# One hybrid decoder layer on one core: the values step of two head pairs is put one tick later

## The chip, the cores and the metric

The kernel runs on one core of a Trainium2 chip. The metric is the device time of one execution in microseconds (us). Five engines matter here: PE (TensorE, the matrix engine), ACT (ScalarE), DVE (VectorE), POOL (GpSimd) and SP (SyncE, which does nothing here but issue transfers). Transfers go through two queues that the profile counts: q1 holds what SP issues, q0 what POOL issues.

## What is computed

One decoder layer on 256 positions of width 2048, in float32. Two kinds of attention with 16 heads each read slices of one projection, and each head has 64 columns:

```python
q_a, k_a, v_a, q_b, k_b, v_b, f_b = jnp.split(rmsnorm(x, pre_mix_g) @ w_in, cuts, axis=-1)
# group A: causal window of 128, 2 key heads for 16 query heads, ALiBi, a learned sink per head
p = jnp.exp(s - m); p = p / (jnp.sum(p, -1) + jnp.exp(sink - m)); o_a = p @ v_a
# group B ("fox"): causal, with per-head forget gates
c = lax.cumsum(log_sigmoid(f_b + b_forget), axis=1)
s = q_b @ k_b.T * scale + c[t] - c[s];  o_b = softmax(s) @ v_b
mix = concatenate([rmsnorm(o_a, grp_swa_g), rmsnorm(o_b, grp_fox_g)]) @ w_out
x = x + rmsnorm(mix, post_mix_g)
# then a feed-forward block of width 5632 with a short causal convolution:
x = x + rmsnorm((gelu(gate) * val) @ w_down, post_ffn_g)
```

## The kernel before

**Numbers.** Each float32 operand of a product is split into a high part and the rest (`hi`, `lo`, names that end in `h`, `l` or `hi`, `lo`), and a product is three matmul passes: high by high, high by low, low by high. ACT makes the high part with a copy, DVE the rest with a subtraction. A 512 KB weight tile is loaded by SP (`raw`, five buffers), cast by ACT (`whi`, L168) and completed by DVE (`wlo`, L171). A `raw` buffer is free for the next load when its `wlo` has been made, so SP's queue of loads follows DVE.

**Order of the work.** PE's order is written out by hand: it is the order in which the program calls. The other engines' instructions are placed by the scheduler of the tile framework. Attention is interleaved with the projections: `proj_T` (matmuls at L309 and L314) calls `tick()` four times in each half of a projection (after the third and the sixth high step, in the pass of the low parts, and at the end), and `later(n, f)` puts a step off by n ticks. What falls on one tick is called in the order in which it was registered.

**A head pair.** `attend` makes four steps for two heads at a time: `tables` (POOL writes the additive mask into `p`; in the fox group this needs a load `cb` of the summed gates), `scores` (PE, L531, three passes with the split keys in `keys`; then DVE maxima, ACT exponentials, DVE normalisation into `p`), `transposes` (PE turns `p` round, L566, three 128x128 blocks for each of the two heads; ACT then casts `ph` and DVE subtracts `pl`, L368 and L369), and `pv`, the values step (PE multiplies by the values, L578 and L580 in the first group, L590 and L592 in the fox group; ACT and DVE bring the result to `oT`, and its squares in `sqo` are added up by POOL, L607 or L609). `ph` and `pl` have one buffer each: the next pair's may be written once this pair's values step has read them. The four steps take their PSUM banks with the tag `att` from four buffers in turn.

**The stages.** Pairs are taken two at a time, m = 0 and 1. `stages(n, m)` gives the ticks of scores, transposes and values: n, n+6+3m, n+9+4m. So the transposes of pair m = 1 and the values step of pair m = 0 fall on the same tick, n+9. The first group ("swa") has pairs 0 to 7 (g = 0 to 3), the fox group pairs 0 to 7 as well, which write `oT` 8 to 15.

**Between the groups.** The gates' running sum is made by PE (L721), copied by DVE (L724), written by SP to the tensor `c_dram` (L725) and read back by SP as `cb`, spread over the partitions (L634). POOL makes the fox tables from it (L639, L641, L645) and afterwards scales the first fox keys (L498); ACT and DVE split these (L368, L369, `keys`), and PE's first fox scores (L531) follow.

**Transfers on the side.** For the feed-forward block, the kernel builds sums of weight rows in DRAM during attention: SP copies rows to tensors `t` (L87, 1 MB each), and POOL adds other rows to them with accumulating transfers (L94, `accum_op`). POOL's instructions are taken in order, so an L94 that stands behind a waiting L609 is issued after it.

Of the kernel before, what the change touches and what calls it, by code (L numbers as in the profile page):

```python
# [34 lines left out]
def hybrid_layer(ctx: ExitStack, tc: tile.TileContext, x, pre_mix_g, w_in, b_forget, sinks,  # L35
# [16 lines left out]
    def bank(tag="acc"):  # L52
        return ps.tile([P, 512], F32, tag=tag, bufs=4, name="bank_" + tag)
# [245 lines left out]
    def proj_T(w, c0, banks):  # L299

        for v in (0, 2):
            parts = [w_split(w_load(w_rows(w, u * 4, 4, c0, 256), 4, 256), still=True)
                     for u in (v, v + 1)]
            steps = [(u, a) for u in range(2) for a in range(4)]

            def high(u, a):
                kt = (v + u) * 4 + a
                for m, b in enumerate(banks):
                    pe.matmul(b, parts[u][0][:, a, m * P:(m + 1) * P], hT[:, kt, :],  # L309
                              start=(kt == 0), stop=(kt == KT - 1))  # L310

            def low(u, a):
                for m, b in enumerate(banks):
                    pe.matmul(b[:, 256:512], parts[u][1][:, a, m * P:(m + 1) * P],  # L314
                              hT[:, (v + u) * 4 + a, 0:256], start=False, stop=False)

            for n, (u, a) in enumerate(steps[:-1]):
                high(u, a)
                if n in (2, 5):
                    tick()  # L320
            for n, (u, a) in enumerate(steps):
                low(u, a)
                if n == 4:
                    tick()
            high(*steps[-1])
            tick()
# [40 lines left out]
    def split(hi, lo, src):  # L367
        act.copy(hi, src)  # L368
        dve.tensor_tensor(lo, src, hi.bitcast(F32), op=ALU.subtract)  # L369

    with tc.tile_pool(name="mixp", bufs=1) as mp:
# [37 lines left out]
        def scratch():  # L409
            rot[0] += 1  # L410
            i = 6 + rot[0] % 10
            return scr[:, i * 256:(i + 1) * 256]
# [80 lines left out]
        def evac_sum(b, dst, row):  # L493

            c = scratch()
            act.copy(c, b[:, 256:512])
            dve.tensor_tensor(dst, b[:, 0:256], c, op=ALU.add)
            pool.tensor_tensor(dst, dst, row, op=ALU.mult)  # L498

        def q_pair(b):  # L500
            q = scratch()
            evac_sum(b, q, rowq)
            qh = ap.tile([P, 256], F32R, tag="qh", bufs=6, name="qh")
            ql = ap.tile([P, 256], F32R, tag="ql", bufs=6, name="ql")
            split(qh, ql, q)
            return qh, ql

        def k_pair(b, i):
            k = scratch()
            evac_sum(b, k, rowk)  # L510
            split(khi[i], klo[i], k)
# [106 lines left out]
        def swa_pair(p, q, at):  # L618
            def table(t):
                for e in range(2):  # L620
                    slope = 2.0 ** (-8.0 * (2 * p + e + 1) / H)
                    pool.tensor_scalar(t[:, e, 0:256], dist, -slope, None, op0=ALU.mult)
                    pool.tensor_scalar(t[:, e, 256:384], dist[:, P:256], -slope, None,
                                       op0=ALU.mult)

            attend(p, q, p // 4, lambda t: vpa[:, t, p // 4, :], table, 2 * p, True, at,
                   True)
# [3 lines left out]
        def fox_pair(p, q, ki, at):  # L631
            def table(t):
                cb = ap.tile([P, 2, 256], F32, tag="cb", bufs=2, name="cb")
                sp.dma_start(cb.rearrange("p e k -> p (e k)"),  # L634
                             c_dram[2 * p:2 * p + 2, :].rearrange("e k -> (e k)")
                             .partition_broadcast(P))
                for e in range(2):
                    h = 2 * p + e
                    pool.tensor_scalar(t[:, e, 0:256], cb[:, e, :], -1.0, cq[:, 1, h:h + 1],  # L639
                                       op0=ALU.mult, op1=ALU.add)  # L640
                    pool.tensor_scalar(t[:, e, 256:384], cb[:, e, 0:P], -1.0, cq[:, 0, h:h + 1],  # L641
                                       op0=ALU.mult, op1=ALU.add)

                v = t[:, :, P:384]
                pool.affine_select(out=v, in_=v, compare_op=ALU.is_ge, fill=NEG, base=0,  # L645
                                   pattern=[[0, 4], [-1, P]], channel_multiplier=1)

            attend(8 + p, q, ki, lambda hl, t: vpb[:, hl, t, p, :], table, 2 * p, False, at)

        def stages(n, m):  # L650
            return n, n + 6 + 3 * m, n + 9 + 4 * m


        def kv_a():
# [21 lines left out]
        for g in range(4):  # L676
            if g == 0:
                b2 = bq0
            else:
                b2 = [bank(), bank()]  # L680
                proj_T(w_in, g * 256, b2)
            for m in range(2):
                swa_pair(2 * g + m, q_pair(b2[m]), stages(7 + 8 * g, m))


        z = ap.tile([P, 2, H], F32, tag="z", name="z")
        for p0, npair, cols in ((0, 3, 384), (3, 3, 384), (6, 2, 272)):
            b2 = [bank(), bank()]
# [55 lines left out]
        for g in range(4):  # L744
            bq = [bank(), bank()]
            proj_T(w_in, 1280 + g * 256, bq)
            qs = [q_pair(b) for b in bq]
            bk = [bank(), bank()]
            proj_T(w_in, 2304 + g * 256, bk)
            for m in range(2):  # L750
                ki = (2 * g + m + 2) % NK
                k_pair(bk[m], ki)
                fox_pair(2 * g + m, qs[m], ki, stages(6, m))


        later(stages(6, 1)[2] + 4, lambda: group_rstd(1, rstd_b))
        mix_sb = main.tile([P, 2, D], F32, tag="y", name="mix_sb")
        mix = [[mix_sb[:, t, n * 512:(n + 1) * 512] for n in range(4)] for t in range(2)]
# [643 lines left out]
```

## Time and profile before

| what | value |
|---|---|
| median of 3 runs | 1056.29 us (1055.24 to 1056.49) |
| the profiled execution, its own time | 1056.47 us |
| its span in the trace | 1054.7 us, so 1.8 us lie around it |
| mean granted PE clock | 0.996 |
| PE busy | 1040.4 us, 99% of the span |
| DVE, ACT, POOL busy | 840.8, 660.5, 268.0 us |

The profiled execution stands 0.18 us above the median. Times inside the trace count from the start of the span. A row of the timeline gives the start, the length, the engine, the line, the operation, output and input, and how many instructions are taken together; in square brackets stands how long the engine was idle before it and what released it.

### The profile page before, as it was taken

To read this page: it belongs to the slowest core of one execution; us is meant where nothing else is said; L and a number is where in the kernel's file an instruction comes from. 1 tells how busy PE (TensorE), PEld (TensorE's weight loads), DVE (VectorE), ACT (ScalarE), POOL (GpSimd) and SP (SyncE) were. 2 spreads that over 40 slices of the span, in tenths; PEclk is the share of its full clock that TensorE was granted. 3 is DMA by queue.
4 is the path that set the end of the run, shared out by engine and by line. 5 is a ranking of instruction groups with operands and counts; after the bars stand their busy time and mean duration, and the time that the engine had idled before them with its cause. 6 is when DMAs were issued, how large, how long until landed. Compare 5 with 4: busy or idle time off the path is not lost.

```text
span 1054.7 us, 16573 instructions
## 1 busy us (share of the span) xinstructions
PE 1040.4 (99%) x5854; PEld 907.1 (86%) x5854; DVE 840.8 (80%) x1371; ACT 660.5 (63%) x1126; POOL 268.0 (25%) x312
## 2 busy tenths in 40 slices
PE   9999999999999999999999999999999999999996
PEld 7889988888889988888888888888888888888885
DVE  5988887787467888778877799867788788779996
ACT  6767666676655865566656675646555666567771
POOL 3254325442022224232232000013223223210004
PEclk9999999999999999999999999999999999999998
DMA  8978999988872899899999796899999999969893
GB/s 282 318 240 289 296 300 304 358 251 299 318 260 68 263 250 270 222 253 258 230 244 265 262 406 192 288 237 222 284 229 243 244 233 265 232 223 384 293 410 131
DMA packets 177470, 279.98 MB, mean 265 GB/s; under 512 B 9052, under 2 KB 133244, under 8 KB 176124
## 3 DMA queue, kind: packets, MB, share of 16 engines
q1 hardware_dynamic: 162432, 249.51, 69.3%
q0 software_dynamic: 13952, 26.74, 17.8%
q10 hardware_dynamic: 1004, 2.68, 0.6%
q8 instruction: 46, 0.75, 0.3%
q14 instruction: 36, 0.29, 0.1%
HBM read 274.55 MB, written 57.69 MB: 315 GB/s over the span
## 4 chain that ended last, share of the span: by engine, by line
PE 93%; DVE 2%; DMA 2%; POOL 1%; ACT 1%; issue 1%; SPq 0%; DVEq 0%; POOLq 0%; ACTq 0%
PE bank_acc L340 16%; PE bank_att L340 14%; PE bank_acc L365 12%; PE bank_att L1044 12%; PE bank_acc L346 8%; PE bank_acc L1044 7%; PE bank_att L346 7%; PE bank_acc L309 7%; PE bank_acc L314 4%; PE bank_att L531 1%; PE bank_att L566 1%; DMA gbc_ffn<-in_post_ffn_g_dram 1%; DVE wlo L171 1%; PE bank_acc L1002 1%; POOL y_sb L1307 1%
## 5 line engine op out<-in xcount | busy, mean ns | idle before, releaser
L171 DVE TENSOR_TENSOR wlo<-raw,whi 128x1024 fp32r<-128x1024 f32 (+3 forms) x271 | 334.2, 1245 | 94.6 <-ACT whi L168 86.9
L168 ACT CAST whi<-raw 128x1024 fp32r<-128x1024 f32 (+3 forms) x270 | 273.7, 1029 | 103.5 <-issue 45.0
L963 POOL TENSOR_TENSOR room<-room,rowf 128x256 f32<-128x256 f32 x88 | 95.8, 1109 | 331.6 <-DVE room L962 329.8
L340 PE MATMUL bank_acc<-hT,whi 128*128 128x512 f32 x736 | 173.3, 390 | 0.0
L340 PEld LDWEIGHTS bank_acc<-hT,whi 128*128 128x128 f32 x736 | 136.4, 188 | 27.4
L340 PE MATMUL bank_att<-hT,whi 128*128 128x512 f32 x640 | 150.6, 390 | 0.0
L340 PEld LDWEIGHTS bank_att<-hT,whi 128*128 128x128 f32 x640 | 118.7, 188 | 23.9
L967 ACT ACTIVATE room<-room,cw 128x256 f32<-128x256 f32 x88 | 52.5, 601 | 65.3 <-POOL room L963 65.0
L346 PEld LDWEIGHTS bank_acc<-hT,wlo 128*128 128x128 f32 x736 | 89.3, 188 | 2.0
L346 PE MATMUL bank_acc<-hT,wlo 128*128 128x256 f32 x736 | 89.8, 279 | 0.0
L309 PE MATMUL bank_acc<-hT,whi 128*128 128x512 f32 x352 | 88.0, 395 | 0.0
L1044 PE MATMUL bank_att<-whi,G 128*128 128x512 f32 x258 | 87.9, 389 | 0.0
L365 PE MATMUL bank_acc<-whi,oT 128*128 128x512 f32 (+1 forms) x272 | 81.8, 379 | 0.0
L369 DVE TENSOR_TENSOR wlo<-raw,whi 128x1024 fp32r<-128x1024 f32 (+1 forms) x66 | 71.4, 1102 | 10.3 <-ACT whi L368 9.6
L346 PEld LDWEIGHTS bank_att<-hT,wlo 128*128 128x128 f32 x640 | 77.6, 188 | 1.7
L346 PE MATMUL bank_att<-hT,wlo 128*128 128x256 f32 x640 | 77.9, 279 | 0.0
L973 DVE SCALAR_TENSOR_TENSOR room<-room,cw 128x256 f32<-128x256 f32 x88 | 59.2, 676 | 22.9 <-ACT room L967 22.9
L368 ACT CAST whi<-raw 128x1024 fp32r<-128x1024 f32 (+1 forms) x66 | 61.7, 953 | 23.2 <-issue 5.7
L309 PEld LDWEIGHTS bank_acc<-hT,whi 128*128 128x128 f32 x352 | 63.3, 188 | 11.6
L365 PEld LDWEIGHTS bank_acc<-whi,oT 128*128 128x128 f32 x272 | 50.2, 188 | 9.3
L1044 PEld LDWEIGHTS bank_att<-whi,G 128*128 128x128 f32 x258 | 48.4, 188 | 10.1
L365 PE MATMUL bank_acc<-wlo,oT 128*128 128x512 f32 (+1 forms) x136 | 51.2, 377 | 0.0
(269 smaller groups left out, 1757.3 us busy)
## 6 DMA issues: line engine op xcount, KB each, us to landing
raw<-in_w_up_dram SPq DMA_DIRECT2D x176, 512.0 KB, 5.6
raw<-in_w_in_dram SPq DMA_DIRECT2D x51, 512.0 KB, 6.4
raw<-in_w_down_dram SPq DMA_DIRECT2D x45, 512.0 KB, 6.9
raw<-in_w_out_dram SPq DMA_DIRECT2D x32, 512.0 KB, 7.0
t<-in_w_down_dram POOLq DMA_DIRECT2D x28, 512.0 KB, 9.2
raw<-t SPq DMA_DIRECT2D x26, 512.0 KB, 6.6
t<-t POOLq DMA_DIRECT2D x18, 512.0 KB, 8.6
extra<-t SPq DMA_DIRECT2D x14, 512.0 KB, 6.7
```

Of the source, the lines that this page charges most:

```text
L168: i1 = act.copy(hi[:, cs], raw[:, cs])
L171: i2 = dve.tensor_tensor(lo[:, cs], raw[:, cs], hi[:, cs].bitcast(F32), op=ALU.subtract)
L309: pe.matmul(b, parts[u][0][:, a, m * P:(m + 1) * P], hT[:, kt, :], start=(kt == 0), stop=(kt == KT - 1))
L340: pe.matmul(b, parts[u][0][:, a, m * P:(m + 1) * P], hT[:, kt, :], start=(kt == 0), stop=(kt == KT - 1))
L346: pe.matmul(b[:, 256:512], parts[u][1][:, a, m * P:(m + 1) * P], hT[:, kt, 0:256], start=False, stop=False)
L365: pe.matmul(b, a, r[:, cols], start=(first and i == 0), stop=(last and i == 2))
L368: act.copy(hi, src)
L369: dve.tensor_tensor(lo, src, hi.bitcast(F32), op=ALU.subtract)
L963: pool.tensor_tensor(u[:, 2:258], u[:, 2:258], rowf, op=ALU.mult)
L967: act.activation(y, u[:, 2:258], AF.Identity, bias=cw[:, 3, ch:ch + 1], scale=cw[:, 2, ch:ch + 1])
L973: dve.scalar_tensor_tensor(y, u[:, 1:257], cw[:, 1, ch:ch + 1], y, op0=ALU.mult, op1=ALU.add)
L1044: pe.matmul(b[:, to] if to else b, a, r[:, cols], start=(first and i == 0), stop=(last and i == 2))
```

## The change

`stages` takes one more argument, which puts the values step one tick later. It is set for pair m = 0 of the last swa group (g = 3, the seventh head pair) and for pair m = 0 of the first fox group (g = 0). One tick lies six or eight projection matmuls further on in PE's order.

```diff
-        def stages(n, m):
-            return n, n + 6 + 3 * m, n + 9 + 4 * m
+        def stages(n, m, more=False):
+            return n, n + 6 + 3 * m, n + 9 + 4 * m + more
...
             for m in range(2):
-                swa_pair(2 * g + m, q_pair(b2[m]), stages(7 + 8 * g, m))
+                swa_pair(2 * g + m, q_pair(b2[m]),
+                         stages(7 + 8 * g, m, g == 3 and m == 0))
...
-                fox_pair(2 * g + m, qs[m], ki, stages(6, m))
+                fox_pair(2 * g + m, qs[m], ki, stages(6, m, g == 0 and m == 0))
```

The changed file has one line more, so lines behind L683 carry a number one higher there.

PE, at the seventh swa pair. L309 and L314 are matmuls of the projection, L578 and L580 the values step of pair 6, L566 the transposes of pair 7:

```order
 L309 MATMUL bank_acc<-hT,whi 128x512 x2
+L566 MATMUL bank_att<-ident,p 128x128 x6
+L309 MATMUL bank_acc<-hT,whi 128x512 x6
 L578 MATMUL bank_att<-ph,vpa 128x512
 L578 MATMUL bank_att<-pl,vpa 128x512
 L580 MATMUL bank_att<-ph,vpa 128x2x128
 L580 MATMUL bank_att<-pl,vpa 128x2x128
-L566 MATMUL bank_att<-ident,p 128x128 x6
-L309 MATMUL bank_acc<-hT,whi 128x512 x14
+L309 MATMUL bank_acc<-hT,whi 128x512 x8
```

The transposes of pair 7 and six matmuls of the projection now stand ahead of the values step of pair 6.

PE, at the first fox pair. L590 and L592 are the values step of fox pair 0, L566 the transposes of fox pair 1:

```order
 L314 MATMUL bank_acc<-hT,wlo 128x256 x10
+L566 MATMUL bank_att<-ident,p 128x128 x6
+L314 MATMUL bank_acc<-hT,wlo 128x256 x6
+L309 MATMUL bank_acc<-hT,whi 128x512 x2
 L590 MATMUL bank_att<-ph,vpb 128x512 x2
 L590 MATMUL bank_att<-pl,vpb 128x512
 L592 MATMUL bank_att<-ph,vpb 128x2x128 x2
 L592 MATMUL bank_att<-pl,vpb 128x2x128
-L566 MATMUL bank_att<-ident,p 128x128 x6
-L314 MATMUL bank_acc<-hT,wlo 128x256 x6
-L309 MATMUL bank_acc<-hT,whi 128x512 x16
+L309 MATMUL bank_acc<-hT,whi 128x512 x14
```

The transposes of fox pair 1 and eight projection matmuls now stand ahead of the values step of fox pair 0.

The scheduler moves instructions of the other engines too. Two of these places are taken up below. First POOL, around the accumulating transfers into `t_74`:

```order
+L94 DMA t_74<-in_w_down_dram 256x512
 L609 TENSOR_TENSOR sqs<-sqs,sqo 128x256
 L94 DMA t_74<-in_w_down_dram 256x512
 L609 TENSOR_TENSOR sqs<-sqs,sqo 128x256 x2
-L94 DMA t_74<-in_w_down_dram 256x512
 L498 TENSOR_TENSOR scr<-scr 128x256 x2
```

There were three L609 around the first transfer, and the second transfer stood behind all of them; now both transfers stand ahead of the last two.

Second SP, around the write of the gates' sums (L725, which is L726 in the changed file) and the loads `cb`:

```order
 L113 DMA raw<-in_w_in_dram 128x4x256 x3
 L87 DMA t_89<-in_w_down_dram 16x16384
-L113 DMA raw<-in_w_in_dram 128x4x256
-L725 DMA c_dram<-scr 16x256
+L113 DMA raw<-in_w_in_dram 128x4x256 x2
+L726 DMA c_dram<-scr 16x256
 L113 DMA raw<-in_w_in_dram 128x4x256
 L634 DMA cb<-c_dram 128x512 x2
```

One weight load more now stands ahead of the write.

## The prediction

> **What bounds the kernel now.** I read the page first, then the list of what PE waited for, then the timeline of PE around the two values steps.
>
> ```profile
> PE 1040.4 (99%) x5854; PEld 907.1 (86%) x5854; DVE 840.8 (80%) x1371; ACT 660.5 (63%) x1126; POOL 268.0 (25%) x312
> PE bank_acc L390 <- DMA x_in<-in_x_dram: 1.3, 1, 1.3
> PE bank_acc L225 <- DVE junk L220: 1.3, 1, 1.3
> PE bank_att L590 <- DVE pl L369: 1.0, 1, 1.0
> PE bank_att L578 <- DVE pl L369: 0.5, 1, 0.5
> 240.00:860.00 620.00, 620.00 (x3417) 539.74 (x3416) 488.90 (x738) 378.55 (x596) 136.86 (x147) 1.00 0.88 253
> ```
>
> PE sets the time: it is busy 99% of the span, and the list names four waits in all. The first two are at the start. The other two are the values steps that the change moves: L590 (fox pair 0) and L578 (swa pair 6) wait for `pl`. The last row (a stretch of 620 us, PE busy in all 620) shows that PE has no gap for a long time behind them. So what PE gains before about 190 us is carried to the end, and so is what it loses.
>
> How large are the two stalls? The timeline of PE has each step disturbed, and some 9 us later the next pair's, which waits for nothing (start, length, what):
>
> ```profile
> 134.81 0.40 PE L578 MATMUL bank_att<-ph,vpa 128*128 128x512 f32 x1
> 135.75 0.50 PE L578 MATMUL bank_att<-pl,vpa 128*128 128x512 f32 x1 [0.54 <-DVE pl L369]
> 136.33 0.82 PE L566 MATMUL bank_att<-ident,p 128*128 128x128 f32 x6
> ...
> 144.38 0.40 PE L578 MATMUL bank_att<-ph,vpa 128*128 128x512 f32 x1
> 145.09 3.34 PE L309 MATMUL bank_acc<-hT,whi 128*128 128x512 f32 x14
> ...
> 179.90 0.63 PE L590 MATMUL bank_att<-ph,vpb 128*128 128x512 f32 x2
> 181.56 0.50 PE L590 MATMUL bank_att<-pl,vpb 128*128 128x512 f32 x1 [1.03 <-DVE pl L369]
> 182.26 0.82 PE L566 MATMUL bank_att<-ident,p 128*128 128x128 f32 x6
> ...
> 188.44 0.62 PE L590 MATMUL bank_att<-ph,vpb 128*128 128x512 f32 x2
> 189.49 0.87 PE L314 MATMUL bank_acc<-hT,wlo 128*128 128x256 f32 x6
> ```
>
> The swa step takes 136.33 - 134.81 = 1.52 us, undisturbed 145.09 - 144.38 = 0.71: it loses 0.81. The fox step takes 182.26 - 179.90 = 2.36, undisturbed 189.49 - 188.44 = 1.05: it loses 1.31. Together 2.12 us, 0.20% of the time. More cannot be gained, since the change removes no instruction.
>
> **Part 1: the swa step.** The transposes of pair 7 (0.57 us from start to start) and six matmuls of 0.235 us come first, so the values step starts about 2.0 us later, at 136.8. Its `pl` was there when PE went on at 135.75. The stall goes, and 0.81 us is gained. The transposes take the two banks behind those of pair 6, so they wait for nothing new. A few matmuls later PE needs the second weight tile of this half projection. It is sooner there by 0.81: transposes from 134.81, 0.57; six matmuls, 1.41; values, 0.71; two matmuls, 0.47; that is 137.97. ACT's cast of that tile:
>
> ```profile
> 136.75 1.03 ACT L168 CAST whi<-raw 128x1024 fp32r<-128x1024 f32 x1
> 124.12 0.37 SPq L113 DMA_DIRECT2D raw<-in_w_in_dram  x1
> raw<-in_w_in_dram SPq DMA_DIRECT2D x1, 512.0 KB, 9.3
> ```
>
> It ends at 137.78, 0.19 us ahead. The load behind this cast (five buffers back) is the one issued at 124.12; it landed 9.3 us later, at 133.4, so it has 3.3 us to spare.
>
> **Part 2: what happens to the 0.81 at the first fox scores.** These are the next place where PE comes close to an input. Rows of PE, ACT, DVE and POOL:
>
> ```profile
> 164.48 0.38 PE L531 MATMUL bank_att<-keys,qh 64*128 64x256 f32 x2
> 164.82 0.34 PE L531 MATMUL bank_att<-keys,qh 64*128 64x256 f32 x4
> 163.49 0.41 ACT L368 CAST keys<-scr 128x256 fp32r<-128x256 f32 x1 [5.80 <-POOL scr L498]
> 163.93 0.51 DVE L369 TENSOR_TENSOR keys<-scr,keys 128x256 fp32r<-128x256 f32 x1 [4.84 <-ACT keys L368]
> 162.72 1.44 POOL L498 TENSOR_TENSOR scr<-scr 128x256 f32<-128x256 f32 x2
> 157.17 0.48 POOL L639 TENSOR_SCALAR p<-cb,cq 128x256 f32<-128x256 f32 x1 [6.85 <-DMA cb<-c_dram]
> 151.81 0.82 SPq L634 DMA_DIRECT2D cb<-c_dram  x2
> 143.54 0.34 SPq L725 DMA_DIRECT2D c_dram<-scr  x1
> 164.50 2.94 ACT L168 CAST whi<-raw 128x1024 fp32r<-128x1024 f32 x3
> ```
>
> (The timeline prints the issues of SP with the queue's name; the others are engines.) The third pass of the scores, at 164.82, needs the low part of the keys, which DVE finishes at 163.93 + 0.51 = 164.44. That is 0.38 us to spare, some 0.33 with the 0.05 us by which PE started behind its release at 181.56. The keys wait for POOL, which works through the tables from 157.17 on, and these wait for `cb`, which waits for the write issued at 143.54. So PE can arrive only 0.33 us sooner, unless that chain is sooner too. Call D the shift of the chain (negative is sooner). After the scores PE is ahead by the lesser of 0.81 and 0.33 - D.
>
> **Part 3: the fox step.** Its own wait goes, but it is not lost from PE's path. The order puts the transposes of fox pair 1 at the place where the values step stood. Banks are taken in turn from four: pair 0's transposes take two, the group sum (L737) the third, so pair 1's first three blocks take the fourth and its second three the first again, which `pl` of pair 0 must have been read from. The row of DVE:
>
> ```profile
> 180.50 1.01 DVE L369 TENSOR_TENSOR pl<-bank_att,ph 128x384 fp32r<-128x384 f32 x2
> ```
>
> One of the two takes half, 0.5, so that bank is free at about 181.05, for PE at 181.10. PE would get there at 179.90 + 0.29 (three blocks of 0.095) = 180.19, less what it is ahead. Between POOL's L498 and this row ACT and DVE run in one chain of casts and exponentials (the last row above, from 164.50 on), so the row moves with D as well. With D = 0: PE is ahead by 0.33, arrives at 179.86 and waits 1.24 us. The values step itself comes eight matmuls later and waits no more. So of the 1.31 saved, 1.24 comes back at the transposes, and the total is 0.33 + 1.31 - 1.24 = 0.40. For other D the sum is 0.40 - D, up to the cap 2.12 (from D = -1.72 on).
>
> **Part 4: what the moved transfers do to D.** POOL's second accumulating transfer stood behind an L609 that waited 16 us for this very pair's squares:
>
> ```profile
> 141.03 0.73 POOL L609 TENSOR_TENSOR sqs<-sqs,sqo 128x256 f32<-128x256 f32 x1 [16.34 <-ACT sqo L602]
> 141.71 0.88 POOL L94 DMA_DIRECT2D t<-in_w_down_dram  x1
> ```
>
> It now goes out right behind the first, at about 119.7. What it did before is seen in the queues' rows for 146:150 (both queues), 137:141, 135:137 and 143:145 (packets, MB, share):
>
> ```profile
> q0 software_dynamic: 222, 0.45, 75.8%
> q1 hardware_dynamic: 230, 0.21, 21.7%
> ...
> q1 hardware_dynamic: 1190, 1.18, 96.1%
> ...
> q1 hardware_dynamic: 70, 0.12, 17.7%
> ...
> q1 hardware_dynamic: 173, 0.36, 45.9%
> c_dram<-scr SPq DMA_DIRECT2D x1, 16.0 KB, 8.3
> ```
>
> While q0 accumulates, SP's queue moves 0.21 MB in 4 us; alone it moves 1.18, 0.295 per us. The 0.21 would take 0.71 us, so the accumulation held SP's queue back by 3.29 us, and in this very time the 16 KB of `c_dram` took 8.3 us. This hold now falls into the time from 123 on, where it pushes weight loads back by as much; SP's queue was nearly idle at 135:137 (0.12 MB, that is 0.41 us of work in 2), which takes up 1.59, and again at 143:145 (0.36 MB, 1.22 us of work in 2), which takes up 0.78. There remain 0.92. And SP's order puts one load of 512 KB (0.524 MB, 1.78 us) ahead of the write. D = -3.29 + 0.92 + 1.78 = -0.59.
>
> What issues the write stays: DVE does the same work ahead of it in another order, and the row of that stretch shows it as good as full (17.57 of 18.5 us):
>
> ```profile
> 125.00:143.50 18.50, 17.96 (x115) 15.40 (x115) 17.57 (x50) 15.31 (x37) 1.56 (x2) 1.00 1.02 299
> ```
>
> The unknown is the transfers. From below, D is -3.29, if neither the load nor the early accumulation delays the chain. From above, it is -3.29 + 3.29 + 1.78 = 1.78, if the idle times of SP's queue take up nothing. I take -0.59, the sum of what the rows show, between the two.
>
> The Trainium skill, "DMA: Bandwidth & Descriptors", section "Latency and other measured facts", gives a transfer issued by SP about 0.6 us to its first byte and a trip to memory up to 2 us at high load; from that an estimate for a write of 16 KB that finds its rings empty is 2.6 us. By that page the write would be back 5.7 us sooner, D would pass its useful limit of -1.72 and the gain would be 2.12. The trace of before does not agree while loads and an accumulation stand in the queues (8.3 us), so I go by the rows; the page speaks for the rival of the full gain only.
>
> **Sum.** 0.40 + 0.59 = 0.99 us gained: 0.81 + 1.31 kept, less 1.13 (1.72 - 0.59) waited at the transposes, and nothing at the scores. 1056.47 - 0.99 = 1055.48 on the profiled execution's own time, which is 0.18 above the median: 1055.30. With the bounds of D the gain lies between 0.40 - 1.78 = -1.38 and 2.12, that is 1057.67 to 1054.17.
>
> **What else moves.** The values step of fox pair 0 is later, and with it everything that reuses `ph` and `pl`: pair 1's can be written only after it. PE would finish it at about 183.1 (181.10 - 0.59, three blocks, six L314 of 0.13, two L309, and 1.05). ACT and DVE then need two casts, two subtractions of 0.5 each and perhaps a `wlo` of 1.2 in between, some 3 us, so 186.1; pair 1's values step stands at 188.44 less the gain, at 187.45. It is hidden with 1.3 us to spare; without that cover PE would wait for `pl` again.
>
> **The rivals.** 0.2% is 2.1 us here: a measurement of this kernel cannot tell less from no change.
>
> *Full gain* (0.25): the chain is at least 1.72 us sooner. For it: the accumulation leaves the very stretch in which the write was slow. Against it: one load more ahead of the write, and loads that were pushed back before. 1056.29 - 2.12 = 1054.17, on the edge of what counts as faster.
>
> *Nothing* (0.15): D is about 0.2, so PE gains 0.2: the swa gain goes at the scores, the fox gain at the transposes. For it: both stalls have the same late `pl`, whatever PE does first. 1056.1.
>
> *Slower* (0.15): the transfers of the accumulation, issued while the weight load of 124.1 is in the queue, and the load ahead of the write delay the keys, and PE waits at the L531 scores, where it never waited. It decides from D = 0.40 on. With D = 1.78 the loss is 1.38: 1057.7. To be slower by 2.1 us, D would have to be 2.5. For it: 0.33 us to spare is little. Against it: the idle stretches of SP's queue.
>
> *The forecast* (0.45): gain 0.5 to 1.6, its own range 1054.7 to 1055.8, with 1055.3 as the middle.
>
> **How the numbers follow.** The range 1054.0 to 1057.5 holds the forecast, the full gain with the spread of the runs, no gain, and most of the slower case; about 0.07 lies below and 0.08 above. Faster by over 2.1 us: 0.11, a part of the full gain, which ends on this bound, and gains that I don't see. Slower by over 2.1 us: 0.07, the far half of the slower case. The rest, 0.82, is within.
>
> **What would show it.** Right: no wait of PE at L578; a wait at L566 for `pl` at about 179.4, of about 1.1 us; none at L590; POOL's second accumulation issued before 121 and q1 busier at 146:150; `cb` landing about 0.6 us sooner. Wrong: a wait of PE at L531 (chain later), a wait at L309 for `whi` near 138 (the pushed load), no wait at L566 at all (chain much sooner), or one of PE behind 190 us.

## The result

| kernel | median (lowest to highest), us | executions |
|---|---|---|
| before | 1056.29 (1055.24 to 1056.97) | 5 |
| changed | 1059.85 (1058.77 to 1061.16) | 5 |

The changed kernel is slower by 3.56 us: the ratio is 1.0037, with the interval 1.0026 to 1.0048. The forecast was 1055.3, with a range up to 1057.5. Both the sign and the range were wrong.

The profiled execution took 1059.85 us, 3.38 more than that of before. First the list of what PE waited for in the changed kernel (two waits at the start left out), and the long stretch behind the attention (busy time of PE, of the weight loads, DVE, ACT and POOL, then the granted clock):

```profile
PE bank_att L531 <- DVE oT L603: 2.1, 1, 2.1
...
PE bank_att L566 <- DVE pl L369: 0.9, 1, 0.9
...
PE bank_att L531 <- ACT keys L368: 0.2, 1, 0.2
240.00:860.00 620.00, 620.00 (x3420) 539.83 (x3419) 490.23 (x739) 379.20 (x601) 139.63 (x149) 1.00 0.88 253
```

The waits at L578 and L590 are gone. In their place stand the one at L566 that was forecast, 0.2 us for the keys, and one nobody had looked for: 2.1 us at the scores of L531 for `oT`, the output of the values step. The stretch of 620 us is as full as before, so nothing was lost there.

The timeline of PE around this wait, first before, then changed:

```profile
193.48 0.38 PE L531 MATMUL bank_att<-keys,qh 64*128 64x256 f32 x2
...
194.40 0.28 PE L531 MATMUL bank_att<-keys,ql 64*128 64x256 f32 x2
...
195.01 0.73 PE L309 MATMUL bank_acc<-hT,whi 128*128 128x512 f32 x2
...
203.44 0.82 PE L566 MATMUL bank_att<-ident,p 128*128 128x128 f32 x6
```

```profile
192.07 0.39 PE L531 MATMUL bank_att<-keys,qh 64*128 64x256 f32 x2
...
192.71 0.44 PE L531 MATMUL bank_att<-keys,qh 64*128 64x128 f32 x3
195.22 0.35 PE L531 MATMUL bank_att<-keys,qh 64*128 64x256 f32 x1 [2.08 <-DVE oT L603]
...
196.02 0.73 PE L309 MATMUL bank_acc<-hT,whi 128*128 128x512 f32 x2
196.59 3.57 PE L314 MATMUL bank_acc<-hT,wlo 128*128 128x256 f32 x16
199.97 3.89 PE L309 MATMUL bank_acc<-hT,whi 128*128 128x512 f32 x16
...
206.02 0.82 PE L566 MATMUL bank_att<-ident,p 128*128 128x128 f32 x6
```

Here the scores of fox pairs 2 and 3 are made, one behind the other. They took 195.01 - 193.48 = 1.53 us before and take 196.02 - 192.07 = 3.95 now, so 2.42 more. And the sixteen L314 behind them take 199.97 - 196.59 = 3.38 us from start to start; the same sixteen take 1.87 in a run without the wait (E4 below). The windows of the changed kernel, 2 us each, say why (PE busy and so on, then the granted clock):

```profile
196.00:198.00 2.00, 2.00 (x11) 1.89 (x10) 1.18 (x10) 1.93 (x10) 0.00 (x0) 0.66 0.93 228
198.00:200.00 2.00, 2.00 (x12) 2.00 (x11) 2.00 (x9) 1.47 (x6) 0.00 (x0) 0.50 1.07 292
```

The clock falls to 0.50 behind the wait; from 200 on it is back (0.99), and before it is 1.00 throughout.

To compare the two traces, one place is needed from which both count: the changed execution reached the first transposes 1.04 us sooner. This differs from execution to execution (54.11 and 53.15 us in two of one and the same kernel, E2 below), and the places that the change moves lie behind it:

```profile
54.37 0.82 PE L566 MATMUL bank_att<-ident,p 128*128 128x128 f32 x6
```

```profile
53.33 0.82 PE L566 MATMUL bank_att<-ident,p 128*128 128x128 f32 x6
```

From that place to the start of the scores at 193.48 (192.07) is 139.11 us before and 138.74 now: the change does save 0.37 us on the way. (Counted from the transposes of swa pair 6, just ahead of the moved steps, it is 0.38, and 0.41 and 0.40 in two more executions, L1 and L2 below.) From there to the transposes of fox pair 2 (the last rows above) it is 9.96 before and 13.95 now: 3.99 lost, of which 2.42 lie at the scores and 1.51 in the L314 at half clock. Together 3.62 lost net, against 3.56 between the medians.

**Why `oT` was late.** DVE's and ACT's rows. The outputs of fox pairs 0 and 1 are read in two halves each, four L603 in all. Of before, the second half of pair 0, the last split of the next keys (L369), and the second half of pair 1:

```profile
184.73 0.49 DVE L603 SCALAR_TENSOR_TENSOR oT<-bank_att,gcol,oT 64x256 fp32r<-64x256 f32 x1
...
190.46 0.43 DVE L369 TENSOR_TENSOR keys<-scr,keys 128x256 fp32r<-128x256 f32 x1 [0.74 <-ACT keys L368]
...
193.58 0.49 DVE L603 SCALAR_TENSOR_TENSOR oT<-bank_att,gcol,oT 64x256 fp32r<-64x256 f32 x1
```

Of the changed kernel, all four reads on DVE, with ACT's cast of the first keys and its first step of pair 0's second half (L601) in between:

```profile
185.30 0.47 DVE L603 SCALAR_TENSOR_TENSOR oT<-bank_att,gcol,oT 64x256 fp32r<-64x256 f32 x1
188.31 0.41 ACT L368 CAST keys<-scr 128x256 fp32r<-128x256 f32 x1 [3.74 <-POOL scr L498]
188.75 0.51 DVE L369 TENSOR_TENSOR keys<-scr,keys 128x256 fp32r<-128x256 f32 x1 [2.99 <-ACT keys L368]
190.39 0.47 ACT L601 ACTIVATE oT<-bank_att,gcol 64x256 fp32r<-64x256 f32 x1
191.16 0.49 DVE L603 SCALAR_TENSOR_TENSOR oT<-bank_att,gcol,oT 64x256 fp32r<-64x256 f32 x1 [1.29 <-ACT sqo L602]
192.94 0.48 DVE L603 SCALAR_TENSOR_TENSOR oT<-bank_att,gcol,oT 64x256 fp32r<-64x256 f32 x1
194.58 0.49 DVE L603 SCALAR_TENSOR_TENSOR oT<-bank_att,gcol,oT 64x256 fp32r<-64x256 f32 x1
```

The values step of pair 0 is later, and so is its output. Its first half is still read ahead of the key splits. Its second half now stands behind them in the order of both engines, and they wait for POOL: ACT sat idle for 3.74 us at its cast, with the second half of pair 0 ready behind it. So that half is read at 191.16 instead of 184.73, the two reads of pair 1 come behind it, and the last ends at 195.07. Before, it ended at 194.07, which is 193.03 counted from the same place: it is 2.04 us later. PE takes four banks in turn, and in the changed order the scores of pair 3 take the banks of the outputs of pairs 0 and 1 (before, only that of pair 1). PE went on 0.15 us behind the end of that read (195.07 to 195.22). Before, it would have been let on at 194.22 and came there by 194.40 at the latest: 0.18 us to spare at most. The read came later by some ten times that cover.

### The profile page after: what moved, and what is told of

It reads as the page before. It is cut to its first block, busy times and chain, and to the rows that moved or that the text cites. A ratio compares the mean times of both kernels' runs of the same rounds, so it can differ in the third digit from the quotient of the medians.

```text
span 1058.1 us, 16575 instructions
## 1 busy us (share of the span) xinstructions
PE 1041.7 (98%) x5854; PEld 907.7 (86%) x5854; DVE 842.9 (80%) x1371; ACT 660.4 (62%) x1126; POOL 270.3 (26%) x312
## 4 chain that ended last, share of the span: by engine, by line
PE 91%; POOL 3%; DVE 2%; DMA 2%; ACT 1%; issue 1%; SPq 0%; DVEq 0%; POOLq 0%; ACTq 0%
PE bank_acc L340 16%; PE bank_att L340 14%; PE bank_acc L365 13%; PE bank_att L1045 12%; PE bank_acc L346 8%; PE bank_acc L1045 7%; PE bank_att L346 7%; PE bank_acc L309 6%; PE bank_acc L314 3%; DMA gbc_ffn<-in_post_ffn_g_dram 1%; PE bank_att L531 1%; PE bank_att L566 1%; PE bank_acc L1003 1%; DVE wlo L171 1%; POOL y_sb L1308 1%
## 5 line engine op out<-in xcount | busy, mean ns | idle before, releaser
L309 PE MATMUL bank_acc<-hT,whi 128*128 128x512 f32 x352 | 88.4, 395 | 0.0
L369 DVE TENSOR_TENSOR wlo<-raw,whi 128x1024 fp32r<-128x1024 f32 (+1 forms) x66 | 71.6, 1105 | 9.1 <-ACT whi L368 8.5
L309 PEld LDWEIGHTS bank_acc<-hT,whi 128*128 128x128 f32 x352 | 63.3, 188 | 11.5
```

## The experiments

Theory A: the late read of the output makes the wait at L531, and the idle time makes the clock fall behind it. Its rival B: the moved transfers (POOL's accumulation, the load ahead of `c_dram`) cost the time, as the slower case of the prediction had it. Stages in the table at the end of this section are taken as above, each from one profiled execution. Each ratio is to executions of before from the same series, with medians of 1055.91 us for E1, E2, E3 and E5 and 1056.40 us for E4, E7, E9 and E10. The mean granted clock of a whole execution also says something of those without a trace: it is 0.996 to 0.998 in all 56 executions of before in these two series.

**E1: the swa edit alone.**

```diff
-                fox_pair(2 * g + m, qs[m], ki, stages(6, m, g == 0 and m == 0))
+                fox_pair(2 * g + m, qs[m], ki, stages(6, m))
```

> The seventh head pair's edit alone (the transfers of POOL and SP move with it, the fox group stays as before). Theory A, late bank: the loss of 3.6 us comes from the fox edit, so this kernel shows no wait at the L531 scores behind 190 us and takes about 1056.0 us: 0.8 gained at L578, of which the first fox scores take back 0.2 to 0.5 and the wait at L590 the rest, because `pl` of fox pair 0 is no sooner. Theory B, transfers: the loss comes from the accumulating transfer and the weight load that were moved, so this kernel is slower than before by 2 us or more.

Measured: 1056.46 us, ratio to before 1.0008 (0.9999 to 1.0017). All moves of transfers come with this edit, and the loss of 3.6 us does not. It gains nothing either. One of its waits:

```profile
PE bank_att L590 <- DVE pl L369: 1.2, 1, 1.2
```

Counted from the transposes of pair 6, PE is 0.77 us ahead of before behind the swa pairs. At the fox scores it waits 0.17 us for the keys and is 0.54 ahead; the scores themselves then take 0.29 longer, since their third pass comes too early for the low part of the keys. The rest is waited at L590 (1.0 before, 1.2 now).

**E2: the fox edit alone.**

```diff
-                swa_pair(2 * g + m, q_pair(b2[m]),
-                         stages(7 + 8 * g, m, g == 3 and m == 0))
+                swa_pair(2 * g + m, q_pair(b2[m]), stages(7 + 8 * g, m))
```

> The first fox pair's edit alone (POOL's transfers and SP's order stay as before). Theory A: the whole loss, about 1059.9 us, with a wait of PE of about 2 us at the L531 scores that DVE's L603 ends, and a stretch of some 3 us behind it in which the granted clock is about half; the wait at L578 is back (0.5). Theory B: no loss, 1055.5 to 1056.5.

Measured: 1059.33, ratio 1.0034 (1.0022 to 1.0046): the whole loss. POOL's and SP's transfers stand in the order of before in it, and the wait of 2.1 us is there. With E1 this leaves B nothing of the loss. The profiled execution was the fastest of its kernel, 1057.68, and it is the one in which the clock did not fall behind the wait (rows of all engines):

```profile
PE bank_att L531 <- DVE oT L603: 2.1, 1, 2.1
196.00:198.00 2.00, 2.00 (x21) 1.84 (x18) 1.18 (x10) 2.00 (x9) 0.00 (x0) 1.00 0.80 223
```

So the wait and the slow clock are two separate terms.

**E3: the change, but the output of fox pair 0 is read ahead of the key splits.** A rule tells the scheduler only that the splits stand behind the second half's L602 (the cast, on ACT) and L603 (the subtraction, on DVE). PE's order and all work stay as they are.

```diff
-            split(khi[i], klo[i], k)
+            for n, ins in enumerate(split(khi[i], klo[i], k)):
+                if behind:
+                    tc.add_manual_dep(
+                        ins.ins, behind[n].ins.name,
...
+                if j == 8:
+                    first_pv.extend(done)
...
-                k_pair(bk[m], ki)
+                k_pair(bk[m], ki, first_pv if g == 1 else ())
```

> The change with one more rule for the scheduler: ACT's and DVE's splits of the keys of the second fox projection may only stand behind the second half of fox pair 0's output (L601 to L603). Nothing else moves. Theory A: DVE ends its last L603 ahead of these scores about 1 us sooner, PE waits 0 to 0.4 us there and the clock stays at 1.00, so the time is 1055.7 to 1056.4. If the wait has another cause, or the clock fell by chance and not through the wait, it stays at 1059 or more.

Measured: 1056.52, ratio 1.0004 (0.9995 to 1.0013). The loss is gone. The lines are seven higher here (L538 is the scores):

```profile
PE bank_att L573 <- DVE pl L369: 0.9, 1, 0.9
PE bank_att L538 <- DVE oT L610: 0.2, 1, 0.2
...
194.08 0.49 DVE L610 SCALAR_TENSOR_TENSOR oT<-bank_att,gcol,oT 64x256 fp32r<-64x256 f32 x1
```

The wait for `oT` falls from 2.1 to 0.2, the L566 wait stays at 0.9, and the scores' stage takes 10.52 us instead of 13.95. The order of these few instructions on ACT and DVE was the cause.

**E10: the reverse, before with a late read.** PE's and SP's orders are those of before; only the second half of pair 0's output is put behind the key splits of the second pair.

```diff
+                if ahead:
+                    tc.add_manual_dep(
+                        ahead[n].ins, ins.ins.name,
...
+                    if j == 8 and r == halves[1]:
+                        first_pv.extend(done)
...
-                k_pair(bk[m], ki)
+                k_pair(bk[m], ki, first_pv if g == 1 and m == 1 else ())
```

> The kernel before, with PE's and SP's order as they were, and one rule: the second half of fox pair 0's output (L601 to L603) may only be made behind the splits of the keys of the second fox projection, as the changed kernel has it. If the late evacuation is the cause, PE waits at the L531 scores for DVE's L603 although no step of PE was moved: DVE has one L603 of 0.5 us and a wait for ACT more ahead of the last one, which then ends about 1.0 us later, at 195.1, and PE needs it at 194.4, so the wait is 0.6 to 0.8 us and the time about 1056.7 to 1057.0. If the moved PE steps themselves are the cause, there is no wait and the time is that of before.

Measured: 1058.26, ratio 1.0019 (1.0010 to 1.0028), with the wait at the expected place (the scores are L539, the read L611 here):

```profile
194.97 0.35 PE L539 MATMUL bank_att<-keys,qh 64*128 64x256 f32 x1 [1.19 <-DVE oT L611]
```

The late read alone makes the wait in a kernel without the change. Its size was expected too small: it is 1.19 us, with 1.9 in the time, of which the stages below show 1.41. The clock stayed at 1.00 behind this shorter wait in the profiled execution. Four of the eleven executions have a mean clock of 0.994 or 0.995, below every one of before, so it may well have fallen in these, which would be part of the 1.9; they have no trace.

**E4: the change with the wait filled.** Ten matmuls that compute nothing that is used are put ahead of the scores of pair 3, in their first bank, so PE is busy while the read is late.

```diff
+                if j == 11:
+                    for _ in range(10):
+                        pe.matmul(sb[0], junk[:, 0:P], junk, start=True, stop=True)
```

> The change, with ten small matmuls on a spare tile (results overwritten, nothing computed is changed) put into PE's order just ahead of the scores of the fourth fox pair, so that PE is busy for about 2.2 us where it waited 2.1 us. The bank is as late as in the change. If the slow clock behind the wait (1.5 us and more) comes from the wait itself, the clock stays at 1.00 in every execution and the time is about 1057.9, that is 2 us over before. If the clock falls by chance or through something else, it stays at 1059.5 and some executions run the matmuls at half speed.

Measured: 1058.36, ratio 1.0021 (1.0012 to 1.0031), 1.49 below the changed kernel. The intervals of the two ratios overlap a little, so the rows and stages have to carry the difference (1.59 in the second stage). PE's rows:

```profile
192.91 2.33 PE L529 MATMUL bank_att<-junk 128*128 128x512 bf16 x9
196.58 2.03 PE L314 MATMUL bank_acc<-hT,wlo 128*128 128x256 f32 x16
198.45 1.76 PE L309 MATMUL bank_acc<-hT,whi 128*128 128x512 f32 x7
```

The L314 start at the same time as in the changed kernel (196.58 and 196.59), so as much is lost at the scores, but they now take 1.87 us and not 3.38, and the clock is 1.00 throughout. All nine executions have a mean clock of 0.996 to 0.998, as before has; in the changed kernel it is 0.995 in three of five. So it was PE's standing idle that lowered the clock. This splits the loss: 1.5 us for the clock, and the remaining 2.0 (1058.36 against 1056.4) for the bank.

**E5: the change with the scores of fox pair 3 one tick later**, so that PE needs the bank later.

```diff
-        def stages(n, m, more=False):
-            return n, n + 6 + 3 * m, n + 9 + 4 * m + more
+        def stages(n, m, more=False, wait=False):
+            return n + wait, n + 6 + 3 * m, n + 9 + 4 * m + more
...
+                fox_pair(2 * g + m, qs[m], ki, stages(6, m, g == 0 and m == 0, g == 1 and m == 1))
```

> The change, and the scores of the fourth fox pair (g = 1, m = 1) one tick later, so that twelve projection matmuls, about 2 us, stand ahead of the matmul that waited 2.1 us. Theory A: the bank is free when PE comes, the wait is 0 to 0.3 us, the clock stays at 1.00, and the time is 1055.6 to 1056.3. If PE's slower clock came by chance, or if something behind these scores was late as well, it stays at 1058 or more.

Measured: 1058.34, ratio 1.0024 (1.0014 to 1.0034). The list has no wait for the bank any more, and the time is not back: a miss. Some of the wait is only hidden: the scores of pair 3 take 1.25 us (195.60 to 196.85), those of pair 2 take 0.84, and PE's second matmul of pair 3 goes on only when DVE has ended its last read at 195.91. And DVE is late itself, since its maxima of pair 2 (L537) stand behind the late read:

```profile
195.42 0.49 DVE L603 SCALAR_TENSOR_TENSOR oT<-bank_att,gcol,oT 64x256 fp32r<-64x256 f32 x1
195.94 0.42 DVE L537 CUSTOM_DVE_ANT_0 p<-bank_att,p 128x256 f32<-128x256 f32 x1
...
210.10 0.50 PE L590 MATMUL bank_att<-pl,vpb 128*128 128x512 f32 x1 [0.75 <-DVE pl L369]
```

Before, that L537 started at 194.42, which is 2.03 us sooner from the common place. What is late on DVE comes back as 0.75 us at the next values step. The stages show 1.83 us of loss in all; the rest of it was not traced.

**E7 and E9: can the forecast's gain be had?** E7 is E3 with the group sum three ticks later, so that the transposes of fox pair 1 take other banks than `pl` is read from; E9 is E7 with E5's later scores.

```diff
-        later(30, lambda: group_rstd(0, rstd_a))
+        later(33, lambda: group_rstd(0, rstd_a))
```

> The change, the output of fox pair 0 ahead of the keys (as in the run before with that rule), and the group sum of the first group (L737) three ticks later, so that fox pair 1's transposes take two fresh banks. The 0.9 us wait at the transposes for `pl` should go. But if the bank of pair 1's output is the next limit, PE comes 0.9 sooner to it and waits about 1.0 us there, so the time stays at 1056 to 1056.6; if nothing else is near, it is 0.9 less than with the rule alone, 1055.3.

> The kernel of the run above, and the scores of the fourth fox pair one tick later, so that PE comes to the bank of pair 1's output some 2 us later. DVE is not late here as it was where the scores alone were moved. If the bank is then free and `pl` of the following pairs is in time, PE keeps the gain: 1054.5 to 1055.5. If the softmax chain of the fourth pair, now begun 2 us later, is late for its transposes or values, a wait of 0.5 to 1 us comes up at L566 or L590 and the time is 1055.8 to 1056.8.

Measured: E7 1055.75, ratio 0.9998 (0.9989 to 1.0007); E9 1056.61, 1.0002 (0.9993 to 1.0011). E7 has no wait at the fox transposes any more, and 0.2 us each for keys, `pl` and `oT`. Its median is the lowest of all, but it cannot be told from before. E9 has a wait of 0.4 at a values step in place of the one for `oT`. With the larger waits removed, what is left to gain is under what a measurement of this kernel can tell.

**L1 to L3: how long the clock stays low.** One profiled execution more each, twice of the changed kernel and once of the fox edit alone, with nothing edited.

> The change itself, looked at again. If the slow clock behind the wait is a matter of the single execution, an execution of 1059 to 1061 us shows about 3 us of half clock behind the 2.1 us wait, and one of about 1058 shows the same wait and full clock.

> The same as the look before: the wait of 2.1 us is there in every execution, the half clock and its 1.5 us only in those of 1059 us and more.

> The fox edit alone, looked at again: its profiled execution took 1057.68 at full clock, below its median of 1059.33. An execution near the median should show the half clock behind the wait; one near 1057.7 should not.

They took 1061.74, 1060.19 and 1059.60 us, all with the wait of 2.1 us and with a slow stretch. PE's rows from 196 on, first L1, then L2:

```profile
196.00:198.00 2.00, 2.00 (x12) 0.50 0.71 227
198.00:200.00 2.00, 2.00 (x12) 0.50 0.91 222
200.00:202.00 2.00, 2.00 (x9) 0.50 1.13 395
```

```profile
196.00:198.00 2.00, 2.00 (x13) 0.50 0.75 220
198.00:200.00 2.00, 2.00 (x16) 0.81 0.97 249
```

The slow stretch is twice as long in L1 as in L2, and L1's execution is 1.55 us longer. So the length of the slow stretch can make much of the spread of these kernels. E2's six executions bear that out: three of up to 1058.86 us have a mean clock of 0.996 or more, three of 1059.81 us and more have 0.995 or less.

The stages, in us (from the first transposes to the scores of fox pair 2, from there to the transposes of pair 2, and from these to the second next ones, at 231 us before):

| kernel | to the scores | scores to transposes | to the second next transposes | sum |
|---|---|---|---|---|
| before | 139.11 | 9.96 | 27.22 | 176.29 |
| changed | 138.74 | 13.95 | 27.25 | 179.94 |
| E1, swa edit alone | 139.43 | 9.96 | 27.23 | 176.62 |
| E2, fox edit alone | 138.30 | 12.35 | 27.25 | 177.90 |
| E3, output read first | 138.71 | 10.52 | 27.26 | 176.49 |
| E10, before with late read | 138.96 | 11.49 | 27.25 | 177.70 |
| E4, wait filled | 138.67 | 12.36 | 27.27 | 178.30 |
| E5, scores later | 139.06 | 10.77 | 28.29 | 178.12 |
| E7, E3 and later sum | 138.18 | 10.48 | 27.26 | 175.92 |
| E9, E7 and scores later | 138.32 | 10.29 | 27.90 | 176.51 |

The loss of the changed kernel and of E2, E4 and E10 stands in the second of these columns. (Of E1's 0.32 in the first, 0.2 is a wait at a swa pair at 59 us, ahead of all moved steps, which the traces of E4 to E10 have as well.)

## Why the prediction was wrong

**The step that failed** is the sentence in the first part that "what PE gains before about 190 us is carried to the end", together with the part on what else moves. The row it rested on (620 us without a gap) begins at 240 us; the stretch from 190 to 240 was taken as covered because no wait stood there. But "no wait" was 0.18 us of slack at the scores of pair 3. The part on what else moves followed what the later values step holds up through `ph` and `pl`, and found it hidden with 1.3 us to spare. That was right: `pl` of pair 1 was there at 185.38, and its values step came at 187.04. It did not follow the step's own output: who reads it, what stands ahead of that read on ACT and DVE now, and who takes the bank next. The scheduler's order does show the second L603 of pair 0 behind the key splits, which waited for POOL before as well. The loss there is 2.04 us for the read less at most 0.18 of slack, plus 1.5 for the clock that falls behind the wait, and the prediction had no term for either.

**Part 1, right.** The stall at L578 is gone, and the values step takes 0.7 us (136.54 - 135.84), as forecast:

```profile
135.84 0.39 PE L578 MATMUL bank_att<-ph,vpa 128*128 128x512 f32 x1
136.54 1.78 PE L309 MATMUL bank_acc<-hT,whi 128*128 128x512 f32 x7
```

No wait for `whi` came up behind it.

**Parts 2 and 3, right in mechanism.** The wait for the keys came, as it does for a chain that is not sooner. It is 0.20 in the list, and the third pass, which needs the low part, starts 0.53 us behind the first and not 0.34 as before, which no list shows. The fox stall moved to the second half of the transposes of pair 1, at 180.08, somewhat smaller than the sum gave for such a chain (1.24):

```profile
162.95 0.39 PE L531 MATMUL bank_att<-keys,qh 64*128 64x256 f32 x2 [0.20 <-ACT keys L368]
163.48 0.45 PE L531 MATMUL bank_att<-keys,qh 64*128 64x256 f32 x4
...
180.08 0.55 PE L566 MATMUL bank_att<-ident,p 128*128 128x128 f32 x3 [0.92 <-DVE pl L369]
```

The gain up to the scores of pair 2 was 0.37 us. The formula 0.40 - D gives that with D = 0.03, and POOL's scaling of the first keys (L498, at 161.71 against 162.72 before) did come 0.03 us later from the common place. The close fit is in part luck: counted from the transposes of pair 6, 0.22 was left behind the first fox scores and 0.16 came at the fox step, where the sum had 0.33 and 0.07 for D = 0.

**Part 4, the term that was mis-sized.** D was put at -0.59 and came out at about zero. Rows of SP's issues and of POOL's first table in the changed kernel:

```profile
142.80 0.33 SPq L726 DMA_DIRECT2D c_dram<-scr  x1
148.09 2.36 SPq L634 DMA_DIRECT2D cb<-c_dram  x2
156.41 1.09 POOL L639 TENSOR_SCALAR p<-cb,cq 128x256 f32<-128x256 f32 x1 [7.89 <-PE bank_acc L309]
c_dram<-scr SPq DMA_DIRECT2D x1, 16.0 KB, 5.3
...
q0 software_dynamic: 95, 0.19, 88.4%
q1 hardware_dynamic: 48, 0.04, 6.5%
```

The write took 5.3 us instead of 8.3: the forecast 3.29 was near for it. So `cb` was issued at 148.09, against 151.81 before: 2.7 us sooner from the same place. But the tables start at 156.41 against 157.17, which is 0.28 later from the same place. (The row names PE as what POOL waited for, but that had long been done.) The read of `cb` itself is the difference: from its issue to the first table it was 5.36 us before and is 8.32 now. It is 8.41 in E1 and 5.20 in E2, so it goes with the moved transfers. The last two rows, of 147:150, show why it could be so: another accumulation fills q0 there, and SP's queue moves 0.04 MB in 3 us. The prediction counted the accumulation that leaves and not the next one, which the sooner read runs into. That this alone made the read longer was not tried. The error cost 0.6 us of the forecast, within the bounds given for D. Of the signs named, POOL's second accumulation was indeed issued before 121 (118.39), but q1 was hardly busier at 146:150 (0.24 MB, 0.21 before), and the tables show no sooner `cb`.

**The rivals.** The slower case had the sign and not the mechanism: it put the loss on the keys, which cost some 0.5 us (0.20 ahead of the scores and 0.28 in them), and E1 and E2 show that the loss does not come with the transfers. "Nothing" describes E1 and E3 well. Among what would prove the forecast wrong, two points came: a small wait at L531 for the keys, which says that the chain was not sooner, and the wait of PE behind 190 us, which made the loss.

## What to carry to other kernels

When a step is put later on one engine, follow its output as far as its inputs: which engine reads it, what stands ahead of that read now, and which later step takes the buffer, with how much to spare. A list of waits shows only the places where the slack is below zero; a step that has 0.2 us left is not in it, and a wait of 0.2 us inside a row of matmuls can be missing too. And a wait on the matrix engine can cost more than its length, when the clock falls behind it.

## What the hardware showed unexpectedly

An idle time of 2.1 us, in a kernel that otherwise keeps PE busy, was followed by a stretch at half clock in four of five profiled executions that have it. In their profiled executions, the waits of before (1.0 us and less, and 1.3 at the start), E10's of 1.19 and the filled one of E4 were followed by none. That does not make waits of 1.2 us safe: beside E10's four executions, one of E5 has a mean clock of 0.994 and one of E9 (1059.90 us) 0.995, with no larger wait than 0.9 listed behind the start in the traces of these two. The length came in steps in the four traces that show it. The row of the window in which the clock falls in the changed kernel, and that in which it comes back, 1 us each:

```profile
196.00:197.00 1.00, 1.00 (x7) 0.82 0.91 231
...
200.00:201.00 1.00, 1.00 (x6) 0.97 1.05 362
```

With a clock of either 1 or 0.5, as the windows on both sides of the edges show it, 0.82 means 0.36 us at half, and 0.97 means 0.06: with the three full ones between, 3.42 us. Worked out in the same way it is 3.40 and 3.42 us in L2 and L3, 6.84 in L1, twice as much, and none in E2. The second column of the stages shows what that costs: 12.35 us in E2, 13.95, 13.90 and 13.88 in the changed kernel, L2 and L3, 15.45 in L1. So the same wait cost 0 or 1.5 us more in two executions of one kernel (E2 and L3), and 1.5, 1.5 or 3.1 in three of the other, with nothing edited in between. The Trainium skill, "TensorE: Matmul & The Clock Gate", section "Part 1: The HAM clock gate", has such a unit: a monitor looks at windows of 3.41 us that run freely, and the clock is either full or half. The lengths agree with that. The Trainium skill's same page, section "HAM oscillation — how this bites in real kernels", has as its rule that PE is to have no idle gaps above about 3.4 us. Here the trace does not agree that shorter ones are safe: 2.08 us was enough in four of five. Which share of a window must be idle was not tried.
